# Token-major gates and branches in a three-block transformer kernel, with moved loads and waits

## The chip, the cores and the metric

The kernel runs on one core of a Trainium2 chip. The metric is device time in microseconds of one execution, as the median of several runs. The engines are named as in the profile: PE is TensorE (PEld its weight loads), DVE is VectorE, ACT is ScalarE, POOL is GpSimd, SP is the engine whose queue issues most of the loads.

## The reference

The input is 256 tokens of 1024 float32 features. Two layers come first: one of retention and one of MoBA attention, each with a squared-ReLU MLP. Then comes a block with four parallel branches, a cross-attention to a memory of 256 tokens and a gated MLP with a convolution. Cut to what the change touches:

```
# MoBA, one block of 256 keys: causal scores within the block
s_own = where(causal, q @ k.T, NEG)
# the four branches
ya = rms_norm(diff_attention(...))
yf = forgetting_attention(...)              # decay from a cumulated log-sigmoid
yc = silu(layer_norm(dwconv31(c_a * sigmoid(c_g))))      # 31 taps, 512 channels
ys = s_b * dwconv3(s_c * s_x)
proj  = einsum('bsnc,ncd->bsnd', stack([ya, yf, yc, ys]), w_branch)
gates = sigmoid(h @ w_gate + b_gate).reshape(B, S, 4, 1024)
x = x + rms_norm(sum(gates * proj, axis=branch) @ w_out)
# the memory, for the cross-attention that follows
m = rms_norm(mem, norm_mem)
```

## The kernel before

Every product with a weight matrix is made of three float32r matmuls: the weight and the activation are each split in a rounded part (`whi`, `xhi`) and the rest (`wlo`, `xlo`), and `mm3` (L250) multiplies high by high, high by low and low by high. Two shapes are in use. `ws` (L255) keeps a 128-column slice of the weight as the stationary operand and streams the 256 tokens, so that its result has features on the partitions. `as_` (L262) keeps 128 tokens stationary and streams 512 columns of the weight, so that its result has tokens on the partitions; `down` (L273) does the same for the projections.

Weights arrive as pieces of 128 x 1024 floats (512 KB), two to a key of `weight_order`. `feed` issues their loads on SP's queue up to `nraw` pieces ahead, `prepare` splits a piece (`whi` on ScalarE, `wlo` on VectorE), and `weights` hands out the two pieces of a key. All large buffers come from one pool of 43 (`b4`), and the PSUM banks that are not accumulators from one of four (`bank`).

The order of work on the engines is the order of the program. `tick` (L206) is called after each stretch of matmuls: it prepares one piece (two when no lane is open and three are waiting), steps each generator in `lanes` and in `light` once, and issues taps of the convolution, which wait in `slow`: `taps` of them, but one if `lanes` holds anything or two pieces were asked for. `drain` ticks until a lane has ended. `later` puts a function one tick off.

The state `done` counts finished keys; a piece may be prepared up to `nprep` (11 in this stage) ahead of it. `as_pair` makes a group of 512 columns of one weight for both halves of the tokens, in four ticks, and counts its two keys as done at the third and the fourth.

The convolution of 31 taps on 4 channel tiles is 124 VectorE instructions in `slow` (`conv_taps`, L938). `conv_lane` (L990) waits until `slow` is empty and then yields from `conv_norm` (L951): transposes of `yc`, statistics, transposes back, eight Silu, and the split into `brh[2]`, `brl[2]`, which branch n = 2 reads. The lane is opened after the branch chunk with j = 16, and `drain(cl)` stands behind the last gate chunk, j = 30.

The four branches lie feature-major in `brh[n]`, `brl[n]`. `MIX_STEPS` alternates chunks of gates (256 gate features each, `ws`) and chunks of branches (four 128-feature tiles, `ws`), with n = 2 last. A gate's bias is the per-partition bias of the sigmoid; two `brh` tiles' products are multiplied by gates, added in `part`, and for n = 2 split into `mx`, the input of the output projection. `mem_norm` is the lane that normalises and transposes the memory.

The first stage starts with loads of x and weights in turn on SP's queue, and `run` writes out the order of single instructions. `rot`, `dec`, `small`, `pp`, `rp` and `fg` are tables; `rot` and `dec` serve retention, the others later stages.

Of the kernel before, what the change touches and what calls it, by code (L numbers as in the profile page):

```python
# [15 lines left out]
ALU = mybir.AluOpType  # L16
# [23 lines left out]
for _n, _w in (("b_glu", 8), ("conv_dw", 4 * 31), ("conv_dw_b", 4), ("ln_g", 4), ("ln_b", 4),  # L40
               ("sc_w", 12), ("b_gate", 32), ("ffn_dw", 3 * 44), ("ffn_dw_b", 44)):
    PP[_n] = _o
    _o += _w
# [56 lines left out]
def tile_model(ctx: ExitStack, tc: tile.TileContext, order, wall, x, mem, gains, gain0, pparam, rparam, w_fg,  # L100
# [33 lines left out]
    def feed(n=None, parts=1):  # L134
        n = n or state["nraw"]
        while state["dma"] < min(npiece, state["prep"] + n):
            raw = b4([128, 1024], "raw")
            for sl in (slice(i * 1024 // parts, (i + 1) * 1024 // parts) for i in range(parts)):
                nc.sync.dma_start(raw[:, sl], wall[state["dma"]][:, sl])
            raws[state["dma"]] = raw, state["now"] + 2  # L140
# [65 lines left out]
    def tick(n=None, taps=3):  # L206
# [8 lines left out]
        rest()  # L215
        for _ in range(1 if lanes or n > 1 else taps):
            if slow and next(slow[0], StopIteration) is StopIteration:
                slow.pop(0)

    def later(f):  # L220

        def g():
            yield
# [38 lines left out]
    def as_(o, w, xh, xl, t, start, stop):  # L262
# [3 lines left out]
        for k in range(4):  # L266
            mm3(o, xh[:, k, ts], xl[:, k, ts], wh[k], wl[k], start and k == 0, stop and k == 3)
            if k == 1 and between:
# [65 lines left out]
    load_x(1, 0)  # L334
    feed(2, 2)
# [29 lines left out]
    def to_T(xn, t, dh, dl):  # L365
        for q in range(2):
# [160 lines left out]
    nc.sync.dma_start(rot, t_rot)  # L527
    for i in range(2):
        nc.sync.dma_start(dec[i], t_dec[:, i * 768:i * 768 + 768])
    feed()  # L530
    nc.sync.dma_start(small, t_small)
    nc.sync.dma_start(pp, pparam)
    nc.sync.dma_start(rp, rparam.broadcast_to([128, NRP]))
    nc.sync.dma_start(fg, w_fg.rearrange("(k p) c -> p k c", p=128))
# [139 lines left out]
    run(x01[0], w2[0], x01[1], w2[1], x01[2])  # L674
    norm = first_r(0)
    run(w3[0], w3[1], x11[0], x11[1], x11[2], norm)
    fill[1][0]()
    norm = first_r(1)
    fill[0][1]()
    norm()  # L680
# [87 lines left out]

    acts, fill = mlp_start(0)
# [44 lines left out]
    def moba_s(hd):  # L814
# [4 lines left out]
        st = stat("mst", 16)  # L819
        for t in range(2):  # L820
            nc.tensor.matmul(ps[:, t * 256:t * 256 + 256], mT[0, i][:, k, tok(t)], mT[1, i][:, k, :],
                             start=True, stop=True)
        for t in range(2):
            o = ps[:, t * 256:t * 256 + 256]
            msk = small[:, C_MASK:C_MASK + 256] if t else small[:, C_MASK + 128:C_MASK + 384]
            nc.vector.tensor_tensor_reduce(e[:, t, :], o, msk, scale=1.0, scalar=NEG, op0=ALU.add, op1=ALU.max,
                                           accum_out=st[:, t:t + 1])
# [310 lines left out]
    def diff_norm():  # L1138
# [20 lines left out]
        for t in range(2):  # L1159
# [3 lines left out]
            yield  # L1163

# [35 lines left out]

    def forget_n(hp):
        e, st = fp[hp]
        nc.vector.reciprocal(st[:, 12:16], st[:, 8:12])
# [483 lines left out]
```

## Time and profile before

| | us |
|---|---|
| median of 3 runs | 1254.6 |
| lowest, highest | 1254.11, 1255.21 |
| the profiled execution | 1255.19 |
| span in its profile, first to last instruction | 1253.2 |
| around the span (1255.19 - 1253.2) | 2.0 |

The profiled execution gives the rows below; its own time is that of its span and what lies around it. Times in a row count from the start of the span. A matmul's duration there overlaps that of its neighbours; the distance from one start to the next is its pitch.

### The profile page before, as it was taken

The page shows a single profiled execution, that of the slowest core. Times are in us where ns is not written, and L with a number is a line of the kernel's source. Part 1 is how long each engine was busy: PE and PEld are TensorE (multiplying, and loading weights), DVE is VectorE, ACT ScalarE, POOL GpSimd, SP SyncE. Part 2 cuts the span into 40 slices and gives each one's busy share as a digit, 9 for nine tenths or more (in the row PEclk, how much of TensorE's full clock was granted, in tenths as well). Part 3 has the DMA queues.
Part 4 walks back from the last instruction along what each step waited for, and adds up shares of the span by engine and source line. Part 5 has one row for each costly group of instructions (what it writes and reads, how often), then busy time and mean ns, then how long its engine had stood idle before and what let it go on. Part 6 is the DMA issues. An engine that isn't in the chain of part 4 may idle for free.

```text
span 1253.2 us, 20071 instructions
## 1 busy us (share of the span) xinstructions
PE 1239.3 (99%) x7888; PEld 1117.4 (89%) x7888; DVE 878.9 (70%) x1553; ACT 681.6 (54%) x1108; POOL 9.3 (1%) x22
## 2 busy tenths in 40 slices
PE   8999999999999999999999999999999999999997
PEld 6888888899988888899998999899999897899996
DVE  6775768755556766765557578788878777588773
ACT  6644445644444765554445546664446566667552
POOL 0000000000000000000000000000000000000000
PEclk9999999999999999999999999999999999999999
DMA  9754464665564535566565554255565654455530
GB/s 356 271 196 156 139 234 148 217 204 182 187 219 134 185 121 182 190 213 191 181 211 177 204 153 147 85 167 171 184 202 202 192 200 163 171 184 187 187 115 34
DMA packets 64351, 226.91 MB, mean 181 GB/s; under 512 B 8193, under 2 KB 8449, under 8 KB 64257
## 3 DMA queue, kind: packets, MB, share of 16 engines
q1 hardware_dynamic: 61808, 217.24, 52.2%
q0 software_dynamic: 2304, 8.39, 2.0%
q8 instruction: 62, 1.02, 0.3%
q14 instruction: 33, 0.26, 0.1%
q10 hardware_dynamic: 144, 0.00, 0.0%
HBM read 224.56 MB, written 1.05 MB: 180 GB/s over the span
## 4 chain that ended last, share of the span: by engine, by line
PE 93%; DVE 3%; ACT 2%; issue 1%; DMA 0%; SPq 0%; DVEq 0%; ACTq 0%
PE ps_ws L251 13%; PE ps_ws L253 13%; PE ps_ws L252 13%; PE ps_as L253 6%; PE ps_as L251 6%; PE ps_as L252 6%; PE mlp L288 4%; PE mlp L287 4%; PE mlp L291 4%; PE ffn L288 1%; PE ffn L287 1%; PE ffn L291 1%; PE ps_br L253 1%; PE ps_br L252 1%; PE ps_br L251 1%; DVE wlo L178 1%
## 5 line engine op out<-in xcount | busy, mean ns | idle before, releaser
L178 DVE TENSOR_TENSOR wlo<-raw,whi 128x1024 fp32r<-128x1024 f32 x404 | 478.1, 1220 | 77.8 <-ACT whi L172 76.7
L172 ACT ACTIVATE whi<-raw 128x1024 fp32r<-128x1024 f32 x404 | 405.6, 1050 | 52.7 <-PE ps_ws L253 14.0
L251 PE MATMUL ps_ws<-xhi,whi 128*128 128x256 f32 x1376 | 391.6, 285 | 0.2 <-ACT fpT L1214 0.2
L252 PE MATMUL ps_ws<-xlo,whi 128*128 128x256 f32 x1376 | 389.3, 283 | 0.0
L253 PE MATMUL ps_ws<-xhi,wlo 128*128 128x256 f32 x1376 | 389.3, 283 | 0.0
L251 PEld LDWEIGHTS ps_ws<-xhi,whi 128*128 128x128 f32 x1376 | 263.8, 192 | 4.5 <-issue 2.3
L252 PEld LDWEIGHTS ps_ws<-xlo,whi 128*128 128x128 f32 x1376 | 263.9, 192 | 1.5
L253 PEld LDWEIGHTS ps_ws<-xhi,wlo 128*128 128x128 f32 x1376 | 263.8, 192 | 0.0
L251 PE MATMUL ps_as<-whi,xhi 128*128 128x512 f32 x352 | 142.1, 404 | 0.7 <-ACT whi L151 0.3
L252 PE MATMUL ps_as<-wlo,xhi 128*128 128x512 f32 x352 | 137.7, 391 | 2.4 <-DVE wlo L178 2.2
L253 PE MATMUL ps_as<-whi,xlo 128*128 128x512 f32 x352 | 138.0, 392 | 0.0
L288 PE MATMUL mlp<-wlo,act 128*128 128x512 f32 x240 | 93.7, 390 | 0.0
L287 PE MATMUL mlp<-whi,act 128*128 128x512 f32 x240 | 93.5, 390 | 0.0
L252 PEld LDWEIGHTS ps_as<-wlo,xhi 128*128 128x128 f32 x352 | 66.2, 188 | 16.9 <-DVE wlo L178 3.3
L253 PEld LDWEIGHTS ps_as<-whi,xlo 128*128 128x128 f32 x352 | 66.1, 188 | 15.3 <-DVE xlo L636 0.9
L251 PEld LDWEIGHTS ps_as<-whi,xhi 128*128 128x128 f32 x352 | 66.2, 188 | 14.3 <-ACT whi L151 0.6
L748 DVE SCALAR_TENSOR_TENSOR relu<-ps_ws,relu 128x512 f32<-128x512 f32 x24 | 16.6, 691 | 87.0 <-ACT relu L747 87.0
L747 ACT ACTIVATE relu<-ps_ws 128x512 f32<-128x512 f32 x24 | 14.4, 598 | 113.8 <-PE ps_ws L253 113.8
L291 PE MATMUL mlp<-whi,act 128*128 128x512 f32 x240 | 74.0, 389 | 0.0
L291 PEld LDWEIGHTS mlp<-whi,act 128*128 128x128 f32 x240 | 45.1, 188 | 9.5
L288 PEld LDWEIGHTS mlp<-wlo,act 128*128 128x128 f32 x240 | 45.1, 188 | 8.6
L287 PEld LDWEIGHTS mlp<-whi,act 128*128 128x128 f32 x240 | 45.2, 188 | 8.6
(427 smaller groups left out, 1632.3 us busy)
## 6 DMA issues: line engine op xcount, KB each, us to landing
raw<-in_wall_dram SPq DMA_DIRECT2D x404, 512.0 KB, 4.1
h<-in_x_dram SPq DMA_DIRECT2D x4, 256.0 KB, 5.8
raw<-in_wall_dram SPq DMA_DIRECT2D x4, 256.0 KB, 4.6
gainln_mix_post<-in_gains_dram POOLq DMA_DIRECT2D x2, 512.0 KB, 4.6
gainln_mlp_pre<-in_gains_dram POOLq DMA_DIRECT2D x2, 512.0 KB, 5.5
gainln_mlp_post<-in_gains_dram POOLq DMA_DIRECT2D x2, 512.0 KB, 7.3
mem<-in_mem_dram POOLq DMA_DIRECT2D x2, 512.0 KB, 7.7
out_dram<-h SPq DMA_DIRECT2D x4, 256.0 KB, 2.0
```

Of the source, the lines that this page charges most:

```text
L172: nc.scalar.activation(hi, raw, AF.Copy)
L178: nc.vector.tensor_tensor(lo, raw, hi.bitcast(F32), op=ALU.subtract)
L251: nc.tensor.matmul(o, ah, bh, start=start, stop=False)
L252: nc.tensor.matmul(o, ah, bl, start=False, stop=False)
L253: nc.tensor.matmul(o, al, bh, start=False, stop=stop)
L287: nc.tensor.matmul(acc[t][n], ah[:, k, ts], wh[k][:, ns], start=st, stop=False)
L288: nc.tensor.matmul(acc[t][n], ah[:, k, ts], wl[k][:, ns], start=False, stop=False)
L291: nc.tensor.matmul(acc[t][n], al[:, k, ts], wh[k][:, ns], start=False, stop=False)
L747: nc.scalar.activation(r, ps, AF.Relu)
L748: nc.vector.scalar_tensor_tensor(r, ps, 0.0, r, op0=ALU.max, op1=ALU.mult)
```

## The change

Gates and branches become token-major: `gate_group` makes 512 gate columns of one branch with `as_pair`, adds the bias, which `gate_bias` loads as a row broadcast to all partitions on POOL's queue, and applies the sigmoid a tick later; `branch_group` multiplies by `as_`, and for n = 2 puts `mixed` two ticks off, which transposes the mixed half back to feature-major. There are 8 groups of gates and 8 of branches. The conv lane is opened after branch group 4, `drain(cl)` stands behind gate group 7, and the memory's load and lane are opened after branch groups 0 and 2 instead of both after chunk j = 20.

MoBA's first 128 queries see 128 keys only. In the forgetting branch the reciprocals are a stage of their own. The differential branch yields once more between its transposes, and the memory's transposes go by halves. `tick` issues `rest()`, which holds the `wlo` of the piece and the next loads, behind the taps. At the start the tables are loaded later, `w3` stands ahead of the first norm, and a piece is prepared ahead of the second one's end. The diff, without the repacking of the weights and parameters on the host:

```diff
-    def feed(n=None, parts=1):
+    def feed(n=None, parts=1, mid=None):
         n = n or state["nraw"]
                 nc.sync.dma_start(raw[:, sl], wall[state["dma"]][:, sl])
+                if mid and sl.start == 0:
+                    mid()
             raws[state["dma"]] = raw, state["now"] + 2
...
                     gs.remove(g)
-        rest()
         for _ in range(1 if lanes or n > 1 else taps):
                 slow.pop(0)
-    def later(f):
+        rest()
+    def later(f, wait=1):
         def g():
-            yield
+            for _ in range(wait):
+                yield
             f()
...
             mm3(o, xh[:, k, ts], xl[:, k, ts], wh[k], wl[k], start and k == 0, stop and k == 3)
-            if k == 1 and between:
+            if k == 2 and between:
                 between.pop()()
...
     feed(1, 2)
-    load_x(1, 0)
-    feed(2, 2)
+    feed(2, 2, lambda: load_x(1, 0))
     load_x(0, 1)
...
-    def to_T(xn, t, dh, dl):
-        for q in range(2):
+    def to_T(xn, t, dh, dl, halves=(0, 1)):
+        for q in halves:
             pt = bank("pt")
...
     dec = [b4([128, 768], f"dec{i}") for i in range(2)]
-    nc.sync.dma_start(rot, t_rot)
-    for i in range(2):
-        nc.sync.dma_start(dec[i], t_dec[:, i * 768:i * 768 + 768])
-    feed()
-    nc.sync.dma_start(small, t_small)
-    nc.sync.dma_start(pp, pparam)
-    nc.sync.dma_start(rp, rparam.broadcast_to([128, NRP]))
-    nc.sync.dma_start(fg, w_fg.rearrange("(k p) c -> p k c", p=128))
+    def load_tables():
+        nc.sync.dma_start(small, t_small)
+        nc.sync.dma_start(pp, pparam)
+        nc.sync.dma_start(rp, rparam.broadcast_to([128, NRP]))
+        nc.sync.dma_start(fg, w_fg.rearrange("(k p) c -> p k c", p=128))
...
     run(x01[0], w2[0], x01[1], w2[1], x01[2])
+    run(*w3)
     norm = first_r(0)
-    run(w3[0], w3[1], x11[0], x11[1], x11[2], norm)
+    run(x11[0], x11[1], x11[2], norm)
     fill[1][0]()
     norm = first_r(1)
+    nc.sync.dma_start(rot, t_rot)
+    prepare(1, force=True)()
+    norm()
     fill[0][1]()
-    norm()
+    for i in range(2):
+        nc.sync.dma_start(dec[i], t_dec[:, i * 768:i * 768 + 768])
     prepare(1, force=True)()
...
+    load_tables()
     acts, fill = mlp_start(0)
...
         st = stat("mst", 16)
-        for t in range(2):
-            nc.tensor.matmul(ps[:, t * 256:t * 256 + 256], mT[0, i][:, k, tok(t)], mT[1, i][:, k, :],
+        nc.gpsimd.memset(e[:, 0, 128:256], NEG)
+        for t in range(2):
+            nk = 128 * (t + 1)
+            nc.tensor.matmul(ps[:, t * 128:t * 128 + nk], mT[0, i][:, k, tok(t)], mT[1, i][:, k, 0:nk],
                              start=True, stop=True)
         for t in range(2):
-            o = ps[:, t * 256:t * 256 + 256]
-            msk = small[:, C_MASK:C_MASK + 256] if t else small[:, C_MASK + 128:C_MASK + 384]
-            nc.vector.tensor_tensor_reduce(e[:, t, :], o, msk, scale=1.0, scalar=NEG, op0=ALU.add, op1=ALU.max,
-                                           accum_out=st[:, t:t + 1])
+            nk = 128 * (t + 1)
+            nc.vector.tensor_tensor_reduce(e[:, t, 0:nk], ps[:, t * 128:t * 128 + nk],
+                                           small[:, C_MASK + 128 - 128 * t:C_MASK + 256], scale=1.0, scalar=NEG,
+                                           op0=ALU.add, op1=ALU.max, accum_out=st[:, t:t + 1])
         nm, b, l, rl = st[:, 2:4], st[:, 4:6], st[:, 6:8], st[:, 8:10]
...
             yield
+            yield
...
+    def forget_r(hp):
+        _, st = fp[hp]
+        nc.vector.reciprocal(st[:, 12:16], st[:, 8:12])
     def forget_n(hp):
         e, st = fp[hp]
-        nc.vector.reciprocal(st[:, 12:16], st[:, 8:12])
         for t in range(2):
...
-    fl = lane(pipe(4, (0, forget_s), (1, forget_e), (2, forget_n), (3, lambda hp: forget_t(hp, 0)),
-                   (4, lambda hp: forget_t(hp, 1)), (5, forget_y), every=2))
+    fl = lane(pipe(4, (0, forget_s), (1, forget_e), (2, forget_r), (3, forget_n),
+                   (4, lambda hp: forget_t(hp, 0)), (5, lambda hp: forget_t(hp, 1)), (6, forget_y), every=2))
     sbt = None
+    gbias = {}
+    def gate_bias(j):
+        b = gbias[j // 2] = b4([128, 2, 512], "gate_bias")
+        r = len(GAINS) + j // 2
+        nc.gpsimd.dma_start(b, gains[r:r + 1, :].rearrange("a (n c) -> a n c", n=2).broadcast_to([128, 2, 512]))
     for i in range(4):
+        if i == 2:
+            gate_bias(0)
         if i % 2 == 0:
...
-    gbuf, part, mx = {}, [], {}
-    state["branch"] = 0
-    def gates(j):
-        if j // 2 % 2 == 0:
-            gbuf["tile", j // 4] = b4([128, 4, 256], "gates")
-        tile = gbuf["tile", j // 4]
-        def evac(ps):
-            for f in range(2):
-                n, ft = GATE_ORDER[j + f]
-                nc.scalar.activation(tile[:, (j + f) % 4, :], ps[:, f * 256:f * 256 + 256], AF.Sigmoid, bias=ppc("b_gate", n * 8 + ft))
-        ws_chunk(("gates", j), evac)
-    def branches(j0, count=4):
-        if j0 % 4 == 0:
-            gbuf["w"] = weights(("branch", j0))
-        w = gbuf["w"]
-        for j in range(j0, j0 + count):
-            n, ft = GATE_ORDER[j]
-            if j % 2 == 0:
-                gbuf["ps"] = bank("ps_br")
-            ps = gbuf["ps"][:, (j % 2) * 256:(j % 2) * 256 + 256]
-            ws(ps, w, (j % 4) * 128, lambda k: brh[n][:, k, :], lambda k: brl[n][:, k, :], width=512)
-            if j % 4 == 3:
+    gbuf, part, mx = {}, {}, {}
+    def gate_group(j):
+        if j % 2 == 0 and j < 6:
+            gate_bias(j + 2)
+        tile = gbuf[j] = b4([128, 2, 512], "gates")
+        def evac(t, ps):
+            nc.vector.tensor_tensor(tile[:, t, :], ps, gbias[j // 2][:, j % 2, :], op=ALU.add)
+            later(lambda: nc.scalar.activation(tile[:, t, :], tile[:, t, :], AF.Sigmoid))
+        as_pair([("cols512", "w_gate_2", 2 * GATE_ORDER[j][1] + GATE_ORDER[j][0], c) for c in range(2)], evac)
+    def branch_group(j):
+        f, n = GATE_ORDER[j]
+        w = weights(("branch", j))
+        g = gbuf.pop(j)
+        if n == 0:
+            part[f] = b4([128, 2, 512], "part")
+        m = part[f]
+        for t in range(2):
+            ps = bank("ps_br")
+            as_(ps, w, brh[n], brl[n], t, True, True)
+            if n == 0:
+                nc.vector.tensor_tensor(m[:, t, :], ps, g[:, t, :], op=ALU.mult)
+            else:
+                nc.vector.tensor_tensor(g[:, t, :], ps, g[:, t, :], op=ALU.mult)
+                nc.vector.tensor_tensor(m[:, t, :], m[:, t, :], g[:, t, :], op=ALU.add)
+            if t == 1:
                 done()
-            if j % 2 == 0:
-                continue
-            g = gbuf["tile", j // 4].rearrange("p a b -> p (a b)")[:, (j % 4 - 1) * 256:(j % 4 + 1) * 256]
-            ft -= 1
-            m = part[ft // 4].rearrange("p a b -> p (a b)")[:, ft % 4 * 256:ft % 4 * 256 + 512]
-            if n == 0:
-                nc.vector.tensor_tensor(m, gbuf["ps"], g, op=ALU.mult)
-            else:
-                nc.vector.tensor_tensor(g, gbuf["ps"], g, op=ALU.mult)
-                nc.vector.tensor_tensor(m, m, g, op=ALU.add)
             if n == 2:
-                a = mx[ft // 2] = act_pair()
-                split(a[0], a[1], tiles(m, 256))
+                if t == 0:
+                    mx[2 * f], mx[2 * f + 1] = act_pair(), act_pair()
+                later(lambda t=t: mixed(f, t), 2)
             tick(taps=1)
+    def mixed(f, t):
+        pt = bank("ps_mx")
+        transposes(pt, part[f][:, t, :])
+        for c in range(2):
+            a = mx[2 * f + c]
+            split(a[0][:, :, tok(t)], a[1][:, :, tok(t)], tiles(pt[:, c * 256:c * 256 + 256]))
...
         for t in range(2):
-            to_T(memn[t], t, mth, mtl)
-            yield
+            for q in range(2):
+                to_T(memn[t], t, mth, mtl, (q,))
+                yield
         if kind == "gate":
-            gates(j)
-            if j == 6:
+            gate_group(j)
+            if j == 1:
                 drain(*lanes, *light)
-                part.extend(b4([128, 4, 256], f"part{i}") for i in range(2))
-            if j == 30:
+            if j == 7:
                 drain(cl)
         else:
-            branches(j)
-            if j == 16:
+            branch_group(j)
+            if j == 4:
                 cl = lane(conv_lane())
-            if j == 20:
-                ml = lane(mem_norm(mem_load()))
+            if j == 0:
+                gm = mem_load()
+            if j == 2:
+                ml = lane(mem_norm(gm))
     drain(ml)
     acc = [pair("mix0"), pair("mix1")]
-    items = [(weights(("rows2", "w_out_2", c)), *mx.pop(c)) for c in range(4)]
+    items = [(weights(("rows2", "w_out_2", c)), *mx[c]) for c in range(4)]
...
-GATE_ORDER = [(n, ft + f) for ft in range(0, 8, 2) for n in (0, 1, 3) for f in range(2)] + [(2, ft) for ft in range(8)]
-MIX_STEPS = [("gate", 0), ("gate", 2), ("gate", 4), ("gate", 6)]
-for _c in range(6):
-    MIX_STEPS += [("branch", 4 * _c)] + [("gate", 4 * _c + 8 + _i) for _i in (0, 2) if 4 * _c + 8 + _i < 24]
-MIX_STEPS += [("gate", _j) for _j in (24, 26, 28, 30)] + [("branch", 24), ("branch", 28)]
+GATE_ORDER = [(f, n) for f in range(2) for n in (0, 1, 3)] + [(f, 2) for f in range(2)]
+MIX_STEPS = [("gate", 0), ("gate", 1)]
+for _j in range(6):
+    MIX_STEPS += [("branch", _j)] + ([("gate", _j + 2)] if _j < 4 else [])
+MIX_STEPS += [("gate", 6), ("gate", 7), ("branch", 6), ("branch", 7)]
```

## Rows read from the trace of the kernel before

**Rows 1.** The page: span, busy time of each engine, and the DMA total.

```profile
span 1253.2 us, 20071 instructions
...
PE 1239.3 (99%) x7888; PEld 1117.4 (89%) x7888; DVE 878.9 (70%) x1553; ACT 681.6 (54%) x1108; POOL 9.3 (1%) x22
...
DMA packets 64351, 226.91 MB, mean 181 GB/s; under 512 B 8193, under 2 KB 8449, under 8 KB 64257
```

**Rows 2.** Timeline of TensorE: start us, duration us, instruction; gates, then the output projection.

```profile
850.06 0.28 PE L251 MATMUL ps_ws<-xhi,whi 128*128 128x256 f32 x1
...
852.94 0.28 PE L251 MATMUL ps_ws<-xhi,whi 128*128 128x256 f32 x1
...
979.66 0.39 PE L287 MATMUL mix<-whi,act 128*128 128x512 f32 x1
...
981.02 0.39 PE L287 MATMUL mix<-whi,act 128*128 128x512 f32 x1
```

**Rows 3.** Waits (us, times, longest): TensorE's, whole span; SP's queue, 836 to 980.

```profile
PE ps_dyt L314 <- DVE brl L248: 1.1, 1, 1.1
PE pt L314 <- DVE mtl L248: 0.7, 1, 0.7
...
SPq L139 <- DVE wlo L178: 47.1, 18, 4.7
```

**Rows 4.** Timeline of TensorE at the start; brackets: idle before, and what ended it.

```profile
17.38 0.50 PE L252 MATMUL ps_as<-wlo,xhi 128*128 128x512 f32 x1 [0.71 <-DVE wlo L178]
...
26.29 0.50 PE L252 MATMUL ps_as<-wlo,xhi 128*128 128x512 f32 x1 [1.32 <-DVE wlo L178]
```

**Rows 5.** Groups of ScalarE by line, 836 to 968 us: busy, mean ns, idle before.

```profile
L1272 ACT ACTIVATE gates<-ps_ws,pp 128x256 f32<-128x256 f32 x32 | 13.4, 471 | 42.5 <-PE ps_ws L253 37.9 <-DVE yc L947 4.6
```

**Rows 6.** Groups of TensorE by line, whole span: one of the branches' three.

```profile
L251 PE MATMUL ps_br<-brh,whi 128*128 128x256 f32 x128 | 36.4, 284 | 0.0
```

**Rows 7.** Timeline of TensorE: transposes, MoBA's scores, and the convolution's first transposes.

```profile
1000.07 1.04 PE L314 MATMUL pt<-ident,y 128*128 128x128 f32 x8
...
449.35 1.02 PE L821 MATMUL mps<-mT,mT 128*128 128x256 f32 x4
...
936.46 1.04 PE L956 MATMUL ps_ct<-ident,yc 128*128 128x128 f32 x8
```

**Rows 8.** Windows 836 to 900 and 900 to 975 us: sum of busy time.

```profile
sum 139.00, PE 138.30 PEld 138.06 DVE 113.46 ACT 70.35 POOL 1.59; mean PE 69.15 PEld 69.03 DVE 56.73 ACT 35.18 POOL 0.80
```

**Rows 9.** Groups of VectorE by line, 836 to 968 us.

```profile
L947 DVE SCALAR_TENSOR_TENSOR yc<-cu,pp,yc 128x232 f32<-128x232 f32 (+29 forms) x74 | 30.6, 462 | 0.0
...
L1296 DVE TENSOR_TENSOR gates<-ps_br,gates 128x512 f32<-128x512 f32 x8 | 5.5, 686 | 2.2 <-PE ps_br L253 2.2
```

**Rows 10.** Timeline of VectorE around the end of the convolution.

```profile
927.46 0.82 DVE L947 SCALAR_TENSOR_TENSOR yc<-cu,pp,yc 128x226 f32<-128x226 f32 x2
...
941.74 0.69 DVE L960 BATCH_NORM_STATS2 bs<-ps_ct 128x6 f32<-128x512 f32 x1
...
945.65 1.53 DVE L965 TENSOR_SCALAR cxn<-ps_ct,ba,z_ln 128x512 f32<-128x512 f32 x2
947.10 3.49 DVE L178 TENSOR_TENSOR wlo<-raw,whi 128x1024 fp32r<-128x1024 f32 x3
```

**Rows 11.** Timeline of ScalarE there.

```profile
950.12 1.28 ACT L975 ACT_TABLE_LOAD   x1
951.42 2.90 ACT L975 ACTIVATE cxn<-ps_ct,pp 128x128 f32<-128x128 f32 x8
954.18 1.19 ACT L247 ACTIVATE brh<-cxn 128x512 fp32r<-128x512 f32 x2
```

**Rows 12.** The kernel's last matmul (timeline), then windows with the granted clock (PEclk, behind POOL).

```profile
1246.30 0.39 PE L253 MATMUL ffn<-whi,act 128*128 128x512 f32 x1
...
1252.00:1253.20 1.20, 0.00 (x0) 0.00 (x0) 0.00 (x0) 0.00 (x0) 0.00 (x0) 0.50 0.00 0
```

**Rows 13.** Timeline of TensorE: the first transposes of the kernel.

```profile
3.65 1.06 PE L314 MATMUL pt<-ident,h 128*128 128x128 f32 x4
```

More of the change, by code (lines that the diff above doesn't have):

```diff
@@ L40 @@
 for _n, _w in (("b_glu", 8), ("conv_dw", 4 * 31), ("conv_dw_b", 4), ("ln_g", 4), ("ln_b", 4),
-               ("sc_w", 12), ("b_gate", 32), ("ffn_dw", 3 * 44), ("ffn_dw_b", 44)):
+               ("sc_w", 12), ("ffn_dw", 3 * 44), ("ffn_dw_b", 44)):
     PP[_n] = _o
@@ L1569, in weight_order @@
         if kind == "gate":
-            o.append(("gates", j))
+            two("cols512", "w_gate_2", 2 * GATE_ORDER[j][1] + GATE_ORDER[j][0])
         else:
@@ L1621, in _chunk @@
         return w.reshape(4, 128, 512).transpose(1, 0, 2)
-    if kind == "gates":
-        w = np.concatenate([inp["w_gate_2"][:, n * 1024 + ft * 128:n * 1024 + ft * 128 + 128]
-                            for n, ft in GATE_ORDER[key[1]:key[1] + 2]], axis=1)
-        return w.reshape(8, 128, 256).transpose(1, 0, 2)
     if kind == "branch":
-        w = np.concatenate([inp["w_branch_2"][n, :, ft * 128:ft * 128 + 128]
-                            for n, ft in GATE_ORDER[key[1]:key[1] + 4]], axis=1)
-        return w.reshape(4, 128, 512).transpose(1, 0, 2)
+        f, n = GATE_ORDER[key[1]]
+        return inp["w_branch_2"][n, :, f * 512:f * 512 + 512].reshape(4, 128, 512).transpose(1, 0, 2)
     raise KeyError(key)
@@ L1643, in _layout @@
                              per(inp["conv_ln_g_2"]), per(inp["conv_ln_b_2"]), taps(inp["sc_w_2"]),
-                             per(inp["b_gate_2"]), taps(inp["ffn_dw_2"]), per(inp["ffn_dw_b_2"])], axis=1)
+                             taps(inp["ffn_dw_2"]), per(inp["ffn_dw_b_2"])], axis=1)
     rparam = np.concatenate([inp[n] for n in ("b_fgt_2", "diff_norm_2", "lam_q1_2", "lam_q2_2", "lam_k1_2",
                                               "lam_k2_2")])[None, :]
-    gains = np.stack([inp[n] for n in GAINS])
+    b_gate = inp["b_gate_2"].reshape(4, 2, 512)
+    rows = [inp[n] for n in GAINS] + list(np.stack([b_gate[n, f] for f, n in GATE_ORDER]).reshape(4, 1024))
+    gains = np.stack(rows)
     return gains, pparam, rparam, inp["w_in_2"][:, F_G:F_G + 8]
```

## Prediction

> **What bounds the kernel now.** I read the page first: TensorE is busy for 99% of the span, VectorE for 70%, ScalarE for 54% [rows 1]. A busy TensorE means only that no gap is recorded, so next I read the timeline of its matmuls for the pitch from start to start. It is 0.120 us for a 256-column f32r matmul (24 of them in 2.88 us) and 0.227 us for a 512-column one (6 in 1.36 us) [rows 2], well below the durations shown. The kernel is therefore a queue of matmuls at their pitch: fewer or cheaper ones shorten it, and other engines count only where TensorE waits. The waits of TensorE show how little that is: 1.1 us once for `ps_dyt`, 0.7 us once for `pt` [rows 3], and at the start two waits of 0.71 and 1.32 us for `wlo` [rows 4]. So the question is what the change does to the number of matmuls, and whether it makes TensorE wait anywhere that it doesn't now.
>
> **Gates and branches.** Gates: 32 instructions evacuate one gate tile each [rows 5], and a tile takes 8 k times 3 = 24 matmuls of 256 columns: 768 x 0.120 = 92.2 us. The new form has 8 groups x 2 t x 8 k x 3 = 384 of 512 columns: 87.2 us, a gain of 5.0. Branches: three lines of 128 matmuls, one of them shown [rows 6], 384 x 0.120 = 46.1 us, become 192 x 0.227 = 43.6: a gain of 2.5. The 16 new transposes in `mixed` cost 0.11 each (8 in 0.80 us, leaving out the last one's tail) [rows 7]: 1.7 lost. Their input is two ticks old, over 5 us of matmuls, so I cost no wait (0 to 2 us if VectorE is late).
>
> Here the Trainium skill speaks against the change. Its page "TensorE: Matmul & The Clock Gate", section "Back-to-back issue gap", gives the spacing as the columns over the clock plus 2.5 ns: two matmuls of 256 would then save 2.5 ns on becoming one of 512, and 576 pairs 1.4 us (an estimate from that page). The rows differ: 13 ns a pair, 7.5 us in all. The sum goes by the rows.
>
> **VectorE in that stage.** It was busy 113.5 of 139 us [rows 8]. The bias, so far in ScalarE's activation, becomes 16 additions from PSUM, priced by the nearest row (0.69 us [rows 9]): 11 us more. 124 us of about 132 still fits, so nothing on the path; without that room the price is up to 5 us. ScalarE has 32 sigmoids of 0.47 us [rows 5] replaced by 16 wider ones: hidden.
>
> **MoBA.** The four `mps` instructions of a head lie 0.21 us apart (1.02 less the last one's 0.38, over 3) [rows 7]. For t = 0 two of them go from 256 to 128 columns, near the 0.11 of a transpose of that width: 8 x 2 x 0.107 = 1.7 us gained. The `memset` runs on an otherwise idle POOL: nothing, up to 0.5 us if a head waits for its buffer.
>
> **Small waits.** The extra `yield` before the second `ps_dyt`, and the reciprocals a stage earlier, end the 1.1 us wait: 1.1 gained (0 to 1.6). Memory transposes by halves end the 0.7 us wait (0 to 0.7 gained); the memory's load, asked for five branch chunks earlier, takes a wait off ScalarE, off the path. `rest()` behind the taps makes a `wlo` up to three taps (1.1 us) later, with over ten pieces prepared ahead: nothing.
>
> **Start.** `w3` before the norm takes four squares off ScalarE ahead of `whi`, and a forced `prepare` comes before `norm()` and the evacuation. The waits at 17.38 and 26.29 shrink; the second comes back partly, since VectorE still has five 1.14 us subtractions to get through. I take their sum, 2.0, as gained (0.5 to 3.2, with what TensorE loses in refilling). The first `load_x` behind a half piece and the transposes at k = 2 trade about 0.4 us each way: nothing. Moved tables: by their shapes 2.2 MB leave SP's queue ahead of the weights, 12 us at the mean rate of the page [rows 1], and four of them, 0.9 MB or 5 us, pass it at the first boundary. In the steady stages SP's loads wait for buffers to come free, up to 4.7 us at a time [rows 3], and TensorE not for weights, so this lead hides them: nothing (up to 5 us if it were gone). The gate biases are 2 MB more on POOL's queue, asked for two groups ahead: nothing.
>
> Gains so far: 5.0 + 2.5 - 1.7 + 1.7 + 1.1 + 0.7 + 2.0 = **11.3 us** (8 to 14).
>
> **The convolution's end, which the diff does not name.** Branch n = 2 needs `brh[2]`, which `conv_norm` makes after the last tap. A tick issues three taps only when `lanes` is empty and n is 1; a branch tick one. Before, 76 taps are left on VectorE when the gates start (74 shown [rows 9], and two opening ones on another line). Eight gate ticks give 24, each round of one branch chunk and two gate chunks 2 + 12, so that they run out in the fourth round. They do, at 928.28 [rows 10], and the first conv transpose follows at 936.46 [rows 7]: `cl` found `slow` empty.
>
> After, three things slow the taps. In `as_pair`, `done()` falls on the last two ticks; at the fourth three pieces are waiting, n becomes 2, and the tick gives one tap: 10 a group. The first group has one tick less at three, as `fl` is a stage longer: 8. And `mem_norm` is a lane from branch 2 on instead of from the sixth chunk, holding ten ticks at one. Counting 77 steps (75 taps and two empty ends) from the first gate tick: g0 8, g1 10, the drain 3, b0 2, g2 10, b1 2, g3 10, b2 2 make 47; g4 4, b3 2, g5 4 under the memory's lane, 57; b4 2, then b5 2, g6 4, g7 4 with `cl` itself in `lanes`, 69. Eight steps are left when `drain(cl)` starts after the last gate. There tick after tick is issued without a matmul, and the next matmuls (b6) need the conv branch: TensorE stands.
>
> The length, from the end T of the last gate matmul. VectorE: the bias addition 0.7; then, with the tap of the last gate tick, 8 taps at 0.37 (0.82 less 0.45) [rows 10] = 3.0, and 3 `wlo` at 1.14 (3.49 less 1.22, over 2) [rows 10] = 3.4: T + 7.1. First transposes 0.6 to the fourth; then from the statistics to the second `cxn`, 941.74 to 947.18 [rows 10], 5.4: T + 13.1. The first half's second transposes end at about T + 13.0, as its `cxn` comes 0.7 earlier. ScalarE's eight Silu take 2.8 (951.42 to 954.18), the first `brh` 0.7 [rows 11]: T + 16.5, with 0.1 until b6 has its `brl`. The 16 transposes in it were on TensorE's path already (1.6): 15.0 us. Two costs on top. An ACT_TABLE_LOAD of 1.28 stands ahead of the Silu [rows 11], hidden or not: 0.6, from 0 to 1.3. And the clock: after the last matmul of the kernel (1246.30) the granted clock reads 0.50 by 1252 [rows 12], the 1.2 GHz level; TensorE idles longer than that gap here, though transposes fall in between. On it a transpose takes 0.21 us (4 in 1.06 at the start, less a tail of 0.42) [rows 13] instead of 0.11, and the start keeps that pitch from its first matmul to about 5.5 us: 0.8 for transposes and 2.0 for four us of b6 at half speed, 2.8 (0 if it doesn't fall). 15.0 + 0.6 + 2.8 = 18.4; I take **18 us** (14 to 22).
>
> **Sum.** The profiled execution took 1255.2 us, a span of 1253.2 and 2.0 around it. 1255.2 - 11.3 + 18 = 1261.9. It lies 0.6 above the median of the three runs (1254.6), so the median to expect is 1261.3, say 1261.
>
> **Rivals.** (A) *The convolution is done in time*, the other side. What decides is the steps left at the last gate: were there none, and eight ticks for the norm besides, the stall is gone and 1254.6 - 11.3 = 1243 remains. For it: before, the same order left 8 us to spare [rows 7, 10]. Against: the count of ticks. It turns to faster once the stall is under 9 us. (B) *Only the norm is exposed*: if n stays 1 in the groups, eight more taps fit, the taps end with the gates, and some 11 us of chain stay: 1254. (C) *VectorE becomes the bound* under bias additions: its backlog delays the banks by up to 5 us: 1266. For it 124 of 132 us, against it the taps postponed. (D) *The clock alone prices matmuls*, so that two of 256 columns cost one of 512 and the 7.5 us stay away: 1269. The pitches of 0.120 and 0.227 [rows 2] speak against it; it is what the gap rule of the Trainium skill's TensorE page, named above, comes near to.
>
> **How the numbers follow.** The stall as counted: 0.78, from 1255 to 1267 with the bounds of stall and gains, not all at one end. A 0.10, B 0.07, C 0.03, D 0.02. A measurement of this kernel tells about 0.2%, 2.5 us, from no change. Slower: 0.73 of the first case, C and D: 0.78. Same: 0.05 and 0.04 of B: 0.09. Faster: A and the rest of B: 0.13. The range 1252 to 1267 leaves out A, D and the tails, under 0.2.
>
> **What would show it.** In the profile after: a stretch of some 15 to 18 us with TensorE almost empty behind the eighth `ps_as` gate, waiting for `yc` and then `brh`, two groups of eight `ps_ct` transposes in it, and a lower granted clock; 512-column matmuls in gates and branches at 0.227; no 1.1 us wait at `ps_dyt`. Wrong is the forecast if `ps_ct` stands between gates or branches as it does now, or if the gates' banks make TensorE wait for the additions.

## The result, and the profile after

The changed kernel takes 1262.49 us (median of 4 runs, 1262.07 to 1264.32). The kernel before took 1254.89 (1254.11 to 1255.21). The ratio is 1.0064, 95% interval 1.005 to 1.0078: the change costs 7.6 us. The forecast was 1261, from 1252 to 1267, and slower.

The page of the changed kernel first, its span and busy times:

```profile
span 1260.3 us, 19040 instructions
...
PE 1234.8 (98%) x7328; PEld 1089.3 (86%) x7328; DVE 887.2 (70%) x1573; ACT 676.9 (54%) x1095; POOL 13.0 (1%) x34
```

Against [rows 1], TensorE has 560 matmuls fewer and 4.5 us less busy time in a span that is 7 us longer. It has therefore become idle somewhere, and the waits of TensorE over the whole span say where (us in total, times, longest):

```profile
PE ps_ct L965 <- DVE yc L956: 6.5, 1, 6.5
PE ps_ct L317 <- DVE cxn L974: 4.0, 1, 4.0
PE ps_br L254 <- ACT brh L250: 2.8, 1, 2.8
...
PE ps_as L255 <- DVE wlo L180: 1.1, 2, 1.0
PE ps_dyt L317 <- DVE sx L1264: 0.7, 1, 0.7
PE ps_as L254 <- ACT xhi L635: 0.6, 1, 0.6
PE ps_fy L1236 <- ACT fpT L1227: 0.4, 1, 0.4
```

The first three are new, 13.3 us together, and come once each. Of the waits in [rows 3], the 0.7 us at `pt` is gone, and the 1.1 us at `ps_dyt` has become 0.7 us for another releaser, with 0.4 us at `ps_fy` beside it. The timeline of TensorE shows that the three lie in one stretch, with the pitches around it (start, duration, instruction, idle time before):

```profile
931.90 0.39 PE L254 MATMUL ps_as<-whi,xhi 128*128 128x512 f32 x1
...
932.58 0.39 PE L254 MATMUL ps_as<-whi,xhi 128*128 128x512 f32 x1
...
953.67 0.38 PE L965 MATMUL ps_ct<-ident,yc 128*128 128x128 f32 x2
960.58 1.69 PE L965 MATMUL ps_ct<-ident,yc 128*128 128x128 f32 x6 [6.53 <-DVE yc L956]
966.29 1.97 PE L317 MATMUL ps_ct<-ident,cxn 128*128 128x128 f32 x8 [4.02 <-DVE cxn L974]
971.08 0.80 PE L254 MATMUL ps_br<-whi,brh 128*128 128x512 f32 x1 [2.82 <-ACT brh L250]
971.67 0.63 PE L255 MATMUL ps_br<-wlo,brh 128*128 128x512 f32 x1
972.10 0.63 PE L256 MATMUL ps_br<-whi,brl 128*128 128x512 f32 x1
```

Three gate matmuls take 0.68 us, a pitch of 0.227, as in [rows 2]. The last matmul of the eighth gate group is over when the first conv transpose starts, at 953.67. From there sixteen transposes stand alone until 971.08, when b6, the first group of branch n = 2 (branch group 6), starts: 17.4 us. VectorE's timeline of that stretch shows what they waited for:

```profile
953.86 0.69 DVE L1292 TENSOR_TENSOR gates<-ps_as,gate_bias 128x512 f32<-128x512 f32 x1 [1.75 <-PE ps_as L256]
954.47 0.45 DVE L956 SCALAR_TENSOR_TENSOR yc<-cu,pp,yc 128x229 f32<-128x229 f32 x1
954.84 1.22 DVE L180 TENSOR_TENSOR wlo<-raw,whi 128x1024 fp32r<-128x1024 f32 x1
...
958.98 1.91 DVE L956 SCALAR_TENSOR_TENSOR yc<-cu,pp,yc 128x228 f32<-128x228 f32 x5
961.45 0.70 DVE L969 BATCH_NORM_STATS2 bs<-ps_ct 128x6 f32<-128x512 f32 x1 [0.57 <-PE ps_ct L965]
...
965.43 1.53 DVE L974 TENSOR_SCALAR cxn<-ps_ct,ba,z_ln 128x512 f32<-128x512 f32 x2
```

It holds the bias addition, then eight taps (three that alternate with three `wlo`, then five in a row) up to 960.89, then the statistics and the normalisation. ScalarE's timeline continues:

```profile
955.13 1.04 ACT L174 ACTIVATE whi<-raw 128x1024 fp32r<-128x1024 f32 x1
966.32 1.28 ACT L984 ACT_TABLE_LOAD   x1 [10.15 <-DVE cxn L974]
967.61 2.90 ACT L984 ACTIVATE cxn<-ps_ct,pp 128x128 f32<-128x128 f32 x8
970.37 1.18 ACT L250 ACTIVATE brh<-cxn 128x512 fp32r<-128x512 f32 x2
```

And windows over the stretch (length, then busy time and instructions of PE, PEld, DVE, ACT and POOL, the granted clock, and the share and rate of the DMA):

```profile
950.00:957.00 7.00, 4.04 (x19) 3.09 (x17) 5.25 (x8) 4.61 (x6) 0.00 (x0) 1.00 0.74 265
957.00:961.00 4.00, 0.42 (x2) 0.24 (x2) 3.89 (x8) 0.00 (x0) 0.00 (x0) 0.51 0.55 194
...
966.00:971.00 5.00, 1.97 (x8) 1.57 (x8) 0.96 (x2) 4.67 (x11) 0.00 (x0) 0.50 0.00 0
971.00:974.10 3.10, 3.02 (x7) 2.40 (x8) 1.29 (x2) 2.44 (x4) 0.00 (x0) 0.50 0.02 5
974.10:980.00 5.90, 5.90 (x27) 4.85 (x27) 3.08 (x5) 0.00 (x0) 0.00 (x0) 1.00 0.25 89
```

The granted clock reads 0.50, the 1.2 GHz level, from 957 to 974.1. The first branch matmuls run in it at a pitch of 0.43 us. The first 36 of branch n = 2, which are the 24 of b6 and 12 of the group behind it, take 9.71 us.

### The profile page after: what moved, and what is told of

The parts are those of the page before. It is cut to its first block, busy times and chain, and to the rows that moved or that the text cites. A ratio compares the mean times of both kernels' runs of the same rounds, so it can differ in the third digit from the quotient of the medians.

```text
span 1260.3 us, 19040 instructions
## 1 busy us (share of the span) xinstructions
PE 1234.8 (98%) x7328; PEld 1089.3 (86%) x7328; DVE 887.2 (70%) x1573; ACT 676.9 (54%) x1095; POOL 13.0 (1%) x34
## 4 chain that ended last, share of the span: by engine, by line
PE 92%; DVE 3%; ACT 3%; issue 1%; DMA 0%; SPq 0%; DVEq 0%; ACTq 0%
PE ps_ws L254 11%; PE ps_ws L256 11%; PE ps_ws L255 11%; PE ps_as L256 8%; PE ps_as L254 8%; PE ps_as L255 8%; PE mlp L291 4%; PE mlp L294 4%; PE mlp L290 4%; PE ffn L291 1%; PE ffn L290 1%; PE ffn L294 1%; PE ps_br L254 1%; PE ps_br L256 1%; PE ps_br L255 1%; DVE wlo L180 1%
## 5 line engine op out<-in xcount | busy, mean ns | idle before, releaser
L174 ACT ACTIVATE whi<-raw 128x1024 fp32r<-128x1024 f32 x404 | 406.4, 1050 | 93.0 <-DVE wlo L180 16.5
L254 PE MATMUL ps_ws<-xhi,whi 128*128 128x256 f32 x1120 | 318.9, 285 | 0.1
L256 PE MATMUL ps_ws<-xhi,wlo 128*128 128x256 f32 x1120 | 317.0, 283 | 0.0
L255 PE MATMUL ps_ws<-xlo,whi 128*128 128x256 f32 x1120 | 316.9, 283 | 0.0
L254 PEld LDWEIGHTS ps_ws<-xhi,whi 128*128 128x128 f32 x1120 | 214.7, 192 | 3.8 <-issue 2.0
L255 PEld LDWEIGHTS ps_ws<-xlo,whi 128*128 128x128 f32 x1120 | 214.8, 192 | 1.5
L256 PEld LDWEIGHTS ps_ws<-xhi,wlo 128*128 128x128 f32 x1120 | 214.8, 192 | 0.0
L254 PE MATMUL ps_as<-whi,xhi 128*128 128x512 f32 x480 | 192.2, 400 | 0.8 <-ACT xhi L635 0.6
L255 PE MATMUL ps_as<-wlo,xhi 128*128 128x512 f32 x480 | 187.5, 391 | 1.1 <-DVE wlo L180 1.1
L256 PE MATMUL ps_as<-whi,xlo 128*128 128x512 f32 x480 | 187.7, 391 | 0.0
L255 PEld LDWEIGHTS ps_as<-wlo,xhi 128*128 128x128 f32 x480 | 90.3, 188 | 20.2 <-DVE wlo L180 2.0
L752 ACT ACTIVATE relu<-ps_ws 128x512 f32<-128x512 f32 x24 | 14.4, 598 | 113.8 <-PE ps_ws L256 113.8
```

What stands on the lines that cost most here:

```text
L174: nc.scalar.activation(hi, raw, AF.Copy)
L254: nc.tensor.matmul(o, ah, bh, start=start, stop=False)
L255: nc.tensor.matmul(o, ah, bl, start=False, stop=False)
L256: nc.tensor.matmul(o, al, bh, start=False, stop=stop)
L752: nc.scalar.activation(r, ps, AF.Relu)
```

## The experiments

Ratios are to the kernel before on the same chip (1254.7 to 1255.0 in all four sets), with 95% intervals.

**1. Taps in spite of the two lanes.** `cl` and `ml` no longer hold the taps back.

```
-        for _ in range(1 if lanes or n > 1 else taps):
+        for _ in range(1 if n > 1 or any(g not in quiet for g in lanes) else taps):
...
                 cl = lane(conv_lane())
+                quiet.append(cl)
...
                 ml = lane(mem_norm(gm))
+                quiet.append(ml)
```

> The conv lane and the memory's lane no longer ration the taps: a tick gives three taps also while only these two are open. Theory 1 (the taps are rationed by the ticks, and the stall is what is left of them and the norm behind the last gate): by the count of ticks the taps end with the gates of group 5, the first conv transposes stand at the first tick of group 6 and the second at the first tick of group 7, so nothing is left to wait for. 1262.5 less the 17.4 us from 953.67 to 971.08, plus 1.6 for the 16 transposes in it, less 1.5 us of slow matmuls in b6: 1245.2, from 1243 to 1248. Rival (VectorE is full in this stage since it adds the gate biases): the same taps, issued earlier, only push evacuations and wlo back, and less than half of the stall comes back: 1254 or more.

Measured: 1249.28 us, ratio 0.9957 (0.9942 to 0.9972). The stall is gone, and 13.2 us with it, yet the time lies 4 us above the expectation. The waits of TensorE show two new ones:

```profile
PE ps_ct L966 <- DVE yc L957: 1.9, 1, 1.9
...
PE ps_as L255 <- DVE part L1310: 1.2, 1, 1.2
```

The windows of this kernel (columns as above) show VectorE busy for 5.93 of 6 and 3.96 of 4 us around the longer of the two waits. Ahead of them, from 904 to 928 us, it is busy throughout as well: its timeline has the memory's norm there, with up to three taps a tick in between. So it is late with what follows.

```profile
930.00:936.00 6.00, 6.00 (x28) 4.99 (x27) 5.93 (x9) 2.80 (x3) 0.00 (x0) 1.00 0.65 202
936.00:940.00 4.00, 2.06 (x12) 1.62 (x11) 3.96 (x6) 1.10 (x2) 0.00 (x0) 0.91 0.82 308
940.00:943.00 3.00, 3.00 (x10) 2.47 (x9) 2.96 (x5) 1.06 (x1) 0.00 (x0) 0.55 0.73 243
```

The clock falls as well behind that wait, and the 48 gate matmuls that follow take 12.18 us instead of 10.88 (48 at 0.227). So the brake on the taps is the cause of the stall, but taking it off everywhere puts the taps where VectorE has no room.

**2. The memory's lane later.** It is opened after branch group 5 and meets only the last few taps.

```
-            if j == 2:
+            if j == 5:
                 ml = lane(mem_norm(gm))
```

> The memory's lane is opened after branch group 5 instead of 2; its load stays where it is. Theory 1: the ten ticks at one tap move behind most of the taps. By the count of ticks the last tap is issued at the end of gate group 6, the first conv transposes at the first tick of group 7, the second ones in the first tick of the drain. Left behind the last gate: transposes, the table load, eight Silu and a split, about 5 us. 1262.5 - 17.3 + 5 = 1250, from 1247 to 1253. If the memory's lane matters little and the two ticks with two pieces do, or VectorE's load: 1259 or more.

Measured: 1252.2 us, ratio 0.9977 (0.9966 to 0.9987), inside the expected range: 10.3 us come back from one number. What is left of the stall stands in three smaller waits, where the late conv norm now meets the memory's:

```profile
PE ps_br L254 <- ACT brh L250: 1.8, 1, 1.8
...
PE pt L317 <- DVE gates L1292: 1.1, 1, 1.1
PE ps_ct L317 <- DVE mtl L251: 1.0, 1, 1.0
```

**3. The gates without their bias.** ScalarE takes the sigmoid from the bank, and VectorE's 16 additions are gone.

```
-            nc.vector.tensor_tensor(tile[:, t, :], ps, gbias[j // 2][:, j % 2, :], op=ALU.add)
-            later(lambda: nc.scalar.activation(tile[:, t, :], tile[:, t, :], AF.Sigmoid))
+            nc.scalar.activation(tile[:, t, :], ps, AF.Sigmoid)
```

> The gate bias is left out, so the gates' values differ: ScalarE takes the sigmoid straight from PSUM, and VectorE is relieved of 16 additions, 11 us. The ticks are the same. Theory 1: the taps left at the last gate are the same eight, the stall stays within 1 us of 17.4 and the time at 1261 to 1263. Rival (VectorE's load makes the taps late): the relieved VectorE has the taps done earlier, the stall falls by 8 us or more, 1254 or less.

Measured: 1265.95 us, ratio 1.0088 (1.0073 to 1.0103), slower than either theory said. VectorE with 11 us less to do doesn't shorten the stall, but my expectation was wrong too, for the edit moves the taps. No sigmoid is pending in `light` any more, so the drain behind gate group 1 has no tick, and three taps come later. The sigmoid of the last bank now also stands on ScalarE ahead of the last three `whi`. VectorE's timeline behind the last gate:

```profile
956.17 1.22 DVE L180 TENSOR_TENSOR wlo<-raw,whi 128x1024 fp32r<-128x1024 f32 x1 [2.34 <-ACT whi L174]
...
960.32 3.01 DVE L956 SCALAR_TENSOR_TENSOR yc<-cu,pp,yc 128x229 f32<-128x229 f32 x8
```

The last gate matmul is over at 954.40 here, so that the first `wlo` starts 1.77 us behind it, where the changed kernel has 1.17 (954.84 less 953.67). Ten taps instead of eight follow; the third of the three late ones is done just ahead, as no addition stands before it. From the last gate to b6 it is 19.1 us, 1.7 more than in the changed kernel. This run can't price the additions; run 11 can.

**4. Idle matmuls in the drain.** 56 matmuls of the identity in all, whose result is not used, in three groups; TensorE stays busy while it waits.

```
+    def dummies(n):
...
+        for _ in range(n):
+            nc.tensor.matmul(keep[0][:, 0:128], ident, ident, start=True, stop=True)
...
+                dummies(28)
                 drain(cl)
```

> During the stall TensorE multiplies the identity by itself: 28 times before the first conv transposes, 17 times behind them, 11 times behind the second ones, 0.21 us each, sized a little under the three waits of 6.5, 4.0 and 2.8 us. Nothing else changes. If the lowered clock (0.50 from 957.04 to 974.11) is a cost of its own: b6 runs at 0.227 us instead of 0.427 (1.5 us), and the first four transposes of each group take 0.4 us less each: 2.3 us less, 1260.2. If the clock costs nothing beside the wait: 1262.5 or a little more.

Measured: 1261.4 us, ratio 1.0051 (1.0034 to 1.0068). The granted clock stays at 1.00 (windows, columns as above):

```profile
957.00:961.00 4.00, 3.93 (x36) 3.69 (x34) 4.00 (x8) 0.00 (x0) 0.00 (x0) 1.00 0.77 272
```

The same 36 branch matmuls take 8.57 us instead of 9.71. So the clock costs 1.1 us here, half of what was expected of it, and nearly all of that in the branch matmuls: the stretch ahead of b6 is 17.21 us, against 17.41.

**5. The rule on two pieces taken out**, which is rival B made on its own.

```
-        for _ in range(1 if lanes or n > 1 else taps):
+        for _ in range(1 if lanes else taps):
```

> The changed kernel with one rule less: a tick that prepares two pieces issues its three taps all the same; the lanes hold the taps back as before. That is rival B of the prediction made on its own. Theory (the stall is a sum of taps and norm behind the last gate): the eight steps that stood behind the last gate are issued ahead of it, so the stall loses eight taps of 0.37 us, 3.0 us, and the chain of the norm, 14.4 us, stays: 1259.5 (1258 to 1261). Rival (VectorE's queue is full, and taps issued earlier only make everything behind them later): the first ps_ct waits 6.5 us as it does now, and the time stays at 1262.5. Rival B's own price in the prediction was 1254, which took some 11 us for the chain.

Measured: 1259.48 us, ratio 1.0036 (1.0023 to 1.0048), on the expected number. The first conv transposes follow the last gate without a wait for `yc`. The two other waits stay, and from the last gate to b6 it is 12.64 us:

```profile
PE ps_ct L317 <- DVE cxn L974: 6.8, 1, 6.8
PE ps_br L254 <- ACT brh L250: 2.8, 1, 2.8
```

The expected number rested on a chain of 14.4 us, so that hitting it is in part luck. The statistics start 4.7 us sooner behind the last gate than in the changed kernel: besides the eight taps (3.0), one of three `wlo` (1.1) no longer stands ahead of them, and the first transposes run beside the rest. Against that, the 36 branch matmuls take 10.19 us instead of 9.71 at the lower clock. From the last `ps_fy` to the last `mix` matmul the trace is 3.8 us shorter than that of the changed kernel; the medians differ by 3.0.

**6. Both: the later memory lane and no rule on two pieces**, the edits of runs 2 and 5.

> The changed kernel with two of the three brakes on the taps taken off: the memory's lane opened after branch group 5 instead of 2, and the rule on two pieces taken out. Counted by ticks, the last tap falls into branch group 4, the first ps_ct into branch group 5, the second into gate group 6, and nothing is left for the drain behind the last gate. Theory (all the loss is the stall, and what it hid is a gain of some 11 us): no wait over 1 us in the stage, 1245.5 (1244 to 1248). Rival (VectorE or the token-major form costs on its own): waits for the gates' banks or a stretch at 1.2 GHz stay and the time is 1249 or more.

Measured: 1245.96 us, ratio 0.9929 (0.9915 to 0.9942), 8.8 us under the kernel before and 16.5 under the changed one. Both groups of conv transposes now stand between branches or gates without a wait (timeline of TensorE):

```profile
928.27 1.03 PE L965 MATMUL ps_ct<-ident,yc 128*128 128x128 f32 x8
...
940.07 1.03 PE L317 MATMUL ps_ct<-ident,cxn 128*128 128x128 f32 x8
```

In the windows of this stage TensorE is busy throughout at a clock of 1.00, even where VectorE has 31.70 of 32 us to do:

```profile
896.00:928.00 32.00, 32.00 (x143) 26.50 (x142) 31.70 (x50) 16.50 (x18) 0.53 (x1) 1.00 0.65 231
928.00:960.00 32.00, 32.00 (x156) 26.65 (x155) 28.65 (x56) 21.83 (x37) 0.00 (x0) 1.00 0.58 199
```

**7. The MoBA part alone, on the kernel before** (its hunk of the diff).

> The kernel before with the MoBA part alone: the first 128 queries see 128 keys. The prediction took 8 x 2 x 0.107 = 1.7 us off. The trace of the changed kernel suggests 1.0 to 1.3 us, because new short waits of mpt for mp came with it. Expected against before: -1.7 if the matmuls alone decide, -1.0 with the waits; 0 if TensorE was not the bound in that stage.

Measured: 1253.23 us, ratio 0.9987 (0.9978 to 0.9996): 1.5 us gained. A head's four score matmuls take 0.82 us where [rows 7] has 1.02, and eight times 0.20 is 1.6:

```profile
448.45 0.82 PE L823 MATMUL mps<-mT,mT 128*128 128x128 f32 x4
```

**8. The parts at the start alone, on the kernel before** (the hunks of `feed`, `as_`, the first loads, the tables and `run`).

> The kernel before with the parts at the start alone: tables loaded later, w3 ahead of the first norm, a piece prepared ahead of the second one's end, transposes behind k = 2, the first half of a piece ahead of the x tile. The prediction took 2.0 us off (0.5 to 3.2). Its two traces show 2.5 us less at the first squared ReLU. Expected against before: -2.0 to -2.5; rival (the start differs by over 1 us from one execution to the next, and the difference of the traces is that): under 1 us.

Measured: 1253.59 us, ratio 0.999 (0.9982 to 0.9999): 1.2 us gained, less than expected. In the first 60 us TensorE still waits for `wlo` twice; before, these waits were 2.2 us in three, so 1.0 of them went:

```profile
PE ps_as L254 <- DVE wlo L180: 1.2, 2, 1.0
```

The 2.5 us between the two traces that I had gone by held one execution's difference from another: in the trace of this run the first MoBA score starts 1.96 us earlier than before, and that of run 7, which has no edit ahead of it, 0.56 us earlier.

**9. The forgetting and differential parts alone, on the kernel before** (`forget_r`, `pipe` and the second `yield`).

> The kernel before with the forgetting and differential parts alone: the reciprocals as a stage of their own, and one more yield between the two ps_dyt transposes. The prediction took the 1.1 us wait of ps_dyt off. The trace of the changed kernel shows waits of 0.7 us at ps_dyt for sx and 0.4 us at ps_fy for fpT in its place. Expected against before: -1.1 by the prediction, 0.0 (within 0.5) if those two waits took the place of the first.

Measured: 1255.07 us, ratio 1.0002 (0.9993 to 1.0011): nothing. The 1.1 us wait for `brl` is not in this kernel's waits, and the two that take its place sum to the same:

```profile
PE ps_dyt L314 <- DVE sx L1245: 0.7, 1, 0.7
PE ps_fy L1227 <- ACT fpT L1218: 0.4, 1, 0.4
```

**10. The table load brought forward**: a Silu of one column behind the statistics.

```
             nc.vector.bn_aggr(ba[:, 2 * t:2 * t + 2], bs)
+        nc.scalar.activation(stat("early", 4)[:, 0:1], ppc("ln_b", 0), AF.Silu)
```

> The changed kernel with one more instruction: a Silu of one column on ScalarE in the drain, behind the convolution's statistics, so that the table load can run in ScalarE's 10 us of idle time and not between the second ps_ct transposes and the first Silu. Theory (the load waits behind the instruction that needs it, and its 1.28 us lie on the path): the eight Silu start 1.3 us earlier, 1261.2 (1260.5 to 1261.8). Rival (the load would have been on the path anyway, or moves elsewhere): 1262.5.

Measured: 1263.16 us, ratio 1.0068 (1.0056 to 1.0081): the theory fell. The load did move, by some 10 us (ScalarE's timeline):

```profile
956.62 1.28 ACT L971 ACT_TABLE_LOAD   x1
...
967.89 2.90 ACT L985 ACTIVATE cxn<-ps_ct,pp 128x128 f32<-128x128 f32 x8 [9.77 <-PE ps_ct L317]
```

Now the Silu waits for the transposes at 1.2 GHz, which start at 966.73: 1.16 us from the first of them to the Silu. With the load in between it was 1.32 us (966.29 to 967.61). The load had been hidden behind the slow transposes but for 0.16 us, and from the last gate to b6 it is 17.26 us instead of 17.41.

The time doesn't fall by that, because the clock comes back later in this run. Its window from 974 us on (columns as above) still reads 0.70, where the changed kernel reads 1.00:

```profile
974.00:978.00 4.00, 4.00 (x14) 3.13 (x13) 1.22 (x2) 0.00 (x0) 0.00 (x0) 0.70 0.00 0
```

The 36 branch matmuls take 10.67 us, against 9.71 in the changed kernel and 8.57 with the clock kept up. Why the lower clock reaches further into the branches here, no run shows.

**11. Run 6 without the gates' bias.**

> The kernel with the later memory lane and without the rule on two pieces, and the gates' bias left out: the sigmoid reads the bank on ScalarE, and VectorE loses its 16 additions (11 us of work). Counted by ticks, the convolution still ends ahead of branch group 4, so that no stall is behind the last gate in either. Theory (VectorE is not the bound and the additions cost nothing): 1246.0, within 1.5 of the same kernel with its bias. Rival C (VectorE's additions hold the gates' banks): 1244 or less.

Measured: 1245.48 us, ratio 0.9927 (0.9914 to 0.9939), against 0.9929 with the bias. In a kernel without the stall the additions cost nothing that can be measured, and rival C falls.

**12. Runs 4 and 10 together.**

> The changed kernel with both the idle matmuls in the drain (which kept the granted clock at 1.00) and the early Silu (which brought the table load forward). Alone, the first let the Silu start 1.32 us after the first of the second ps_ct transposes, because the table load of 1.28 us then stood between; the second let it start 1.16 us after, because the transposes at 1.2 GHz took that long. Theory (the two cover each other, and only both together free the path): the Silu starts some 0.65 us after that transpose, b6 keeps its 2.4 GHz pitch, and the time is 0.6 us under that of the idle matmuls alone: 1260.8. Rival (something third sets the Silu's start): 1.2 to 1.3 us as before, 1261.4.

Measured: 1260.79 us, ratio 1.0046 (1.0032 to 1.006), on the expected number, though the 0.6 us against run 4 is inside the interval. The trace is clearer than the time. The first of the second transposes starts at 966.82, and ScalarE's timeline has the Silu 0.69 us later:

```profile
967.51 2.90 ACT L987 ACTIVATE cxn<-ps_ct,pp 128x128 f32<-128x128 f32 x8 [9.11 <-DVE cxn L976]
```

From the last gate to b6 it is 16.61 us, where the changed kernel has 17.41, run 4 17.21 and run 10 17.26. Each of the two costs had covered the other: in this chain, removing one alone brought 0.2 us or less, both 0.8.

## Why the prediction was right, point by point

**The stall** was the right mechanism at the right place, for the reason given. Eight taps and three `wlo` stand behind the last gate, as counted, and the last tap ends 7.2 us after it (counted 7.1). The statistics start at 7.8 (7.7), `cxn` ends at 13.3 (13.1), and b6 starts at 17.4 (16.5, and 0.6 for half the table load). Runs 1, 2, 5 and 6 show the cause: they change only the rules on taps or the moment at which the memory's lane opens, and 3 to 16.5 us come back.

**Its size** was 16.5 us by run 6, where the prediction took 18 (14 to 22). The mis-sized term is the clock, 2.8 for 1.1. I had added the transposes' slower pitch and 2.0 us of b6. But the branches' loss is 1.1 (run 4), and the transposes' 0.8 lies in a chain that VectorE and ScalarE set: the stretch ahead of b6 lost 0.2. The table load's 0.6 was a mean of "hidden or not": at 1.2 GHz it was hidden but for 0.16 us (run 10), at 2.4 GHz it stood for 0.63 (1.32 in run 4 less 0.69 in run 12). Counted from the trace, 17.4 less 1.6 for sixteen transposes, plus 1.1, is 16.9. From the last `ps_fy` to the last `mix` matmul the changed kernel's trace has 172.51 us (834.48 to 1006.99) and that of run 6 155.60, which is 16.9 more. The rest lies outside this stage, where one execution differs from another: the two traces reach its start 1.0 us apart, the other way (834.48 and 835.45).

The clock's price isn't one number: in run 10 the same 36 matmuls lost 2.1 us, about the 2.0 that I had taken, and in the changed kernel 1.1. With the table load moved ahead, keeping the clock up is worth 2.4 us in the times (1263.16 for run 10, 1260.79 for run 12). The pitch of 0.21 for a slow transpose came from [rows 13], where the trace's granted clock reads 1.00. The changed kernel has the same pitch at 0.50, so the figure was right, though that row alone did not show the level.

**Gates, branches, `mixed`, memory halves**: 5.0 + 2.5 - 1.7 + 0.7 = 6.5 us were predicted. The prices came from the right rows: the pitch after is 0.227, and four `ps_mx` transposes take 0.35. (8 transposes in 0.80 are 0.10 each, and not 0.11, which is 0.1 us over the sixteen.) From the last `ps_fy` to the last `mix` matmul, the trace before has 164.47 us (835.37 to 999.84) and that of run 6 155.60 (835.45 to 991.05). Twelve gate matmuls, 2.72 us, have moved ahead of that mark in run 6, so that 6.15 us are gained. Rival D falls with it. The gap rule of the Trainium skill's page "TensorE: Matmul & The Clock Gate", section "Back-to-back issue gap", would have left 1.4 us of the 7.5; the rows were right. The section gives that rule for an isolated matmul, which the prediction leaves out, and these stand in long streams.

**MoBA**: 1.5 for 1.7 (run 7). **Start**: 1.2 for 2.0 (run 8). There the step that failed is "I take their sum, 2.0, as gained", although the same paragraph said that the second wait comes back partly: 1.2 of 2.2 us of waits stayed. **Small waits**: nothing for 1.1 (run 9). The step that failed is "end the 1.1 us wait", for it asked what the wait was for and not what comes late next. In run 9 these are `sx` and `fpT`. Moved tables and the loads of the gate biases cost nothing that shows: run 8 has the tables and gains, and in run 6 TensorE waits for no load in the stage of the biases.

**The sum.** The parts measured on their own (MoBA, the start, run 9's 0.4 us of loss, which is inside its interval, and the gates) are 1.5 + 1.2 - 0.4 + 6.15 = 8.5 us, and run 6, which has them all and no stall, gained 8.8. So the gains were 8.8 where 11.3 was predicted, and the stall 16.5 where 18 was: both were taken too large and cancel in part. The mechanism was right; that 1261 came within 1.5 us of 1262.5 is partly luck.

**The rivals.** A (in time, 1243) didn't happen, but run 6 makes it happen, at 1246. B's condition was made in run 5 and gave 1259.5, not 1254. Its chain was priced well: 12.6 us less 1.6 for the transposes is 11. But the clock fell in it too, for which B had nothing (36 branch matmuls in 10.19 us, against 8.57 in run 4), and the gains are 2.5 smaller. C was tested in run 11, and the additions cost nothing there. VectorE does become the bound in places in run 1, by the taps and the memory's norm.

## What to carry to other kernels

Work that a scheduler hands out in portions per tick has a deadline; when an edit changes how many ticks there are, or which rule limits a portion, count the portions left at the deadline before pricing anything else. A change that makes each part cheaper can lose as a whole by one rule that it doesn't name: here two edits of a line each turn 7.6 us of loss into 8.8 of gain. And when two costs end at about the same instant, taking one away shows nothing; only both together do.

## What the runs showed of the hardware

The table load did not use ScalarE's 10.15 us of idle time. It started at 966.32, when the first `cxn` was done, so it stood behind what its Silu waited for; moved ahead by a Silu on data that was there, it ran some 20 ns behind the `whi` before it (run 10). The Trainium skill's page "ScalarE: Activation LUTs", section "What ACT_TABLE_LOAD costs", gives 1283 ns for the load, which the trace agrees with (1.28 us), and a drain of 1380 ns on top, which no run here shows: the Silu follows the end of the load by some 10 ns.

The clock fell not only in the long stall. In run 1 TensorE was busy for 2.06 of the 4 us from 936 to 940, with one wait of 1.9 us among its transposes, and the granted clock then read 0.55 from 940 to 943, while TensorE was busy all the time. A wait of 1.9 us cost another 1.3 in the gates behind it.
